# Forget-gate products before the norm factor's row in their shared bank, the first norm's chain before v's second splits, and a warm-up from a constant

## The chip, the cores and the metric

The kernel runs on one core of a Trainium2 chip. The metric is the device time of one execution in microseconds (us), as the median of several runs. Engines are named as the profile names them: PE (matrix products), PEld (its weight loads), DVE (vector), ACT (scalar), POOL (GpSimd), SP (the queue that issues most transfers).

## The reference, cut to what matters

One decoder layer over 256 tokens of 1024 channels: two attention branches in parallel, a gate that merges them, and a gated feed-forward part with a short convolution.

```python
h = rms_norm(x, attn_norm_g)
proj = h @ w_in           # qa, ka, va, qb, kb, vb, f_logit, g_logit
o_a = causal softmax attention(qa, ka, va)       # 8 heads of 64, RMS norm and partial rotation on q and k
log_f = log_sigmoid(f_logit + b_forget)          # one value per token and head
o_b = softmax(qb.kb/8 + c[t] - c[s]) vb          # c = cumsum(log_f)
gates = sigmoid(g_logit + b_gate)
x = x + (gates0 * (o_a @ w_branch_moba) + gates1 * (o_b @ w_branch_fox)) @ w_out
h2 = rms_norm(x, ffn_norm_g);  u, g = split(h2 @ w_ffn_up)
x = x + (silu(conv(g)) * u) @ w_ffn_down
```

With 256 tokens and blocks of 256 keys the first branch is plain causal attention. The factor of a token's RMS norm is one number, so the kernel multiplies it in after the products: h @ w is rs times (x * g) @ w.

## The kernel before, in words

**Products in parts.** Every large product is made three times in a fast format: a matrix is split into a rounded high part and the remainder as low part (`hi`, `lo`), and high x high, low x high and high x low are added up in PSUM. The weights stream in as `raw` tiles of 1 MB (three buffers). ACT makes the high half (L118), DVE the low half (L119), 1024 columns at a time; such a half is called a split here, and the tiles `whi` and `wlo` have six buffers each. `use` (L125) makes sure that the splits up to five places ahead are written into the program before a split is consumed. The order of the splits is: 8 of the head (`head`, which also hold x), then `qkv` in four matrices of two transfers with two splits each, then the gate and later weights. I number them from 0: 0 to 7 are the head, 8 and 9 are v's first transfer, 10 and 11 v's second, 12 to 15 q of the second branch, 16 to 19 its k, 20 to 23 its v. SP issues a transfer when the last split of the transfer three before it has been read.

**Order.** PE's order is the program's order, written out by hand (L468 to L661). On DVE, ACT, POOL and SP a planner orders the instructions by a modelled readiness and a priority, which is the place in the program; what stands in `with soon()` is taken 45 places earlier. `after(i, j)` keeps i behind j on the same engine, with no wait of its own.

**Around the change.** PE first multiplies a memset tile eight times as a warm-up (L162 to L166). Then come the 8 head steps `project_qk` (L226), the sums of squares of x (L206, in `norm1`), v (L236), q of the second branch (L236), then `turn_qk(qn, 0, 0)` (16 transposes, L284), `forget_a`, `turn_qk(kn, 0, 1)` (16 transposes, L284), and k of the second branch (L236). `norm1` computes the factor `rs` from the sums: L193 on DVE, Ln and Exp on ACT (L194), L195 to L197 on DVE. `finish_qk` needs `rs`: squares on ACT (L248), sums on DVE (L249), a chain like the norm's, products on DVE (L258) and the rotation (L265 to L268); its results `qn` and `kn` go into the transposes.

`forget_a` (L297) takes one PSUM bank of 512 columns. First `rs_row` (L428) lets PE spread `rs` over all partitions in the right half of the bank (four products, L430) and DVE copies that to `rsB` (L431), which the gates use from L451 on. Then PE makes the forget gate's products in the left half (16 matmuls, L302, from `xT`, which two SP transfers bring at L483) and DVE copies them to `fs` (L304), which `forget_b` (L311) reads. `scores` (L374) follow soon after that.

Of the kernel before, what the change touches and what calls it, by code (L numbers as in the profile page):

```python
# [8 lines left out]
F32 = mybir.dt.float32  # L9
F32R = mybir.dt.float32r  # L10
BF16 = mybir.dt.bfloat16
AF = mybir.ActivationFunctionType
ALU = mybir.AluOpType
# [4 lines left out]
P = 128  # L18
S = 256
NT = 2  # L20
D = 1024
KT = D // P
# [6 lines left out]
BIG = 1e30  # L29
HALF = 8  # L30
RB, HB, AHEAD = 3, 6, 5
NWARM = 8
SOON = 45
GAPS = (160, 96)
HEADW = S + 2 * W4
# [7 lines left out]
def decoder_block(ctx, tc, a, out):  # L43
    nc = tc.nc
# [6 lines left out]
    def T(shape, tag, bufs=1, dt=F32):  # L51
        return sb.tile(shape, dt, tag=tag, bufs=bufs, name=tag)

    def bank():
        return ps.tile([P, 512], F32, tag="bank", bufs=8, name="bank")
# [31 lines left out]
    pos = {u: i for i, u in enumerate(units)}  # L87
    split = {}
    loads = {}
    state = {"next": 0, "raw": None}  # L90

    def load(upto):
        while state["next"] <= min(upto, len(units) - 1):
            c, h = units[state["next"]]
            if c[0] == "head":
                k = c[1]
                raw = T([P, 2048], "raw", RB)
                cuts = (0, S + W4, HEADW) if k < 2 else (0, HEADW)
                for s0, s1 in zip(cuts, cuts[1:]):
                    loads[c] = nc.sync.dma_start(raw[:, s0:s1], a["head"][k][:, s0:s1])  # L100
                x, raw = raw[:, 0:S], raw[:, S:HEADW]
                split_x(k, x)
                at, n = 44, 2 if k < 2 else 1
            else:
                at, n = 44 if c[0] == "qkv" else 0, 1
                if h == 0:
                    src = a[c[0]]
                    for j in c[1:]:
                        src = src[j]
                    state["raw"] = T([P, 2048], "raw", RB)  # L110
                    loads[c] = nc.sync.dma_start(state["raw"], src)
                raw = state["raw"][:, h * 1024:(h + 1) * 1024]
            hi = T([P, 1088], "whi", HB, F32R)[:, at:at + 1024]
            lo = T([P, 1088], "wlo", HB, F32R)[:, at:at + 1024]
            w = 1024 // n
            for j in range(n):
                s = slice(j * w, (j + 1) * w)
                nc.scalar.activation(hi[:, s], raw[:, s], AF.Copy)  # L118
                nc.vector.tensor_tensor(lo[:, s], raw[:, s], hi[:, s].bitcast(F32), op=ALU.subtract)  # L119
            if c[0] == "head":  # L120
                square_x(k, x)
            split[c, h] = (hi, lo)
            state["next"] += 1

    def use(c, h):  # L125
        load(pos[c, h] + AHEAD)
        return split.pop((c, h))


# [14 lines left out]
    def split_x(k, x):  # L144
        g = g1[:, k:k + 1]
        if k == 0:
            nc.vector.tensor_scalar_mul(xh[:, k], x, g)
        else:
            nc.scalar.activation(xh[:, k], x, AF.Copy, scale=g)
        nc.vector.scalar_tensor_tensor(xl[:, k], x, g, xh[:, k].bitcast(F32), op0=ALU.mult, op1=ALU.subtract)  # L150

    def square_x(k, x):
        sq = T([P, 512], "sq", 2)[:, 0:S]
        nc.scalar.activation(sq, x, AF.Square)
        if k == 1:
            nc.gpsimd.tensor_tensor(xss[:, 1], xsq[0], sq, op=ALU.add)
        elif k > 1:
            nc.gpsimd.tensor_tensor(xss[:, k % 2], xss[:, (k + 1) % 2], sq, op=ALU.add)
        xsq.append(sq)


    warm = T([P, 512], "sq", 2, BF16)  # L162
    nc.vector.memset(warm, 0.0)
    wp = bank()
    for j in range(NWARM):
        nc.tensor.matmul(wp, warm[:, 0:P], warm, start=True, stop=True)  # L166

    load(5)
    ones1 = T([P, 1], "ones1")
    nc.vector.memset(ones1, 1.0)  # L170
    cst = T([P, 840], "cst")
    ident = cst[:, 0:128]
# [16 lines left out]
    def rsqrt_mean(dst, ss, n, shape, tag, bufs=2):  # L189

        w = T([P, 3] + shape, tag, bufs)
        v, y, t = w[:, 0], w[:, 1], w[:, 2]
        nc.vector.tensor_scalar(v, ss, 1.0 / n, EPS, op0=ALU.mult, op1=ALU.add)  # L193
        i = nc.scalar.activation(t, v, AF.Ln), nc.scalar.activation(y, t, AF.Exp, scale=-0.5)  # L194
        nc.vector.scalar_tensor_tensor(t, v, -0.5, y, op0=ALU.mult, op1=ALU.mult)  # L195
        nc.vector.tensor_tensor(t, t, y, op=ALU.mult)
        nc.vector.scalar_tensor_tensor(dst, t, 1.5, y, op0=ALU.add, op1=ALU.mult)  # L197
        return i

    rs = T([P, NT], "rs")  # L200
    rope = []

    def norm1():
        ssp = bank()
        for t in range(NT):
            nc.tensor.matmul(ssp[:, t:t + 1], xss[:, 1, t * P:(t + 1) * P], ones1, start=True, stop=True)  # L206
        rsqrt_mean(rs, ssp[:, 0:NT], D, [NT], "rsv")

        for i in range(2):
            gr = sm[:, C_GR + 16 * i:C_GR + 16 * (i + 1)][:, None, :].to_broadcast([P, NT, 16])  # L210
            rc = T([P, NT, 16], f"rc{i}")
            rsn = T([P, NT, 16], f"rsn{i}")
            nc.vector.tensor_tensor(rc, cos2[:, :, 0:16], gr, op=ALU.mult)
            nc.vector.tensor_tensor(rsn, cos2[:, :, 16:32], gr, op=ALU.mult)
            rope.append((rc, rsn))
# [4 lines left out]
    def project_qk(k, pts):  # L220
        wh, wl = use(("head", k), 0)
        for m, pt in enumerate(pts):
            rh, rl = wh[:, m * W4:(m + 1) * W4], wl[:, m * W4:(m + 1) * W4]
            for i, (lhs, rhs) in enumerate(((xh, rh), (xl, rh), (xh, rl))):
                for t in range(NT):
                    nc.tensor.matmul(pt[t], lhs[:, k, t * P:(t + 1) * P], rhs, start=(k == 0 and i == 0), stop=(k == KT - 1 and i == 2))  # L226

    def project(m, pt, h):
        for hh in range(2):
            wh, wl = use(("qkv", m - 2, h), hh)  # L230
            for k2 in range(2):
                k = 4 * h + 2 * hh + k2
                rh, rl = wh[:, k2 * 512:(k2 + 1) * 512], wl[:, k2 * 512:(k2 + 1) * 512]
                for i, (lhs, rhs) in enumerate(((xh, rh), (xl, rh), (xh, rl))):
                    for t in range(NT):
                        nc.tensor.matmul(pt[t], lhs[:, k, t * P:(t + 1) * P], rhs, start=(k == 0 and i == 0), stop=(k == KT - 1 and i == 2))  # L236
# [52 lines left out]


    gates = T([P, KT, 2, S], "gates")
    bias = T([P, NH, 384], "bias")
    cc = T([P, NT, NH], "cc")

# [1 line left out]

    def forget_a():  # L297
        fp = bank()
        rs_row(fp[:, S:])
        for k in range(KT):  # L300
            r = slice(32 * (k % 4), 32 * (k % 4 + 1))
            nc.tensor.matmul(fp[r, :S], wfg[:, k], xT[:, k], start=(k < 4), stop=(k >= 4))  # L302
        fs = T([P, 2, 384], "pT", 4)[:, 0, 0:S]
        nc.vector.tensor_copy(fs, fp[:, :S])  # L304
        fg["fs"] = fs

    def forget_b():
# [115 lines left out]
            nc.vector.tensor_tensor(ol[:, b], o2, oh[:, b].bitcast(F32), op=ALU.subtract)  # L423


    rsB = T([P, S], "rsB")

    def rs_row(rp):  # L428
        for t in range(NT):
            nc.tensor.matmul(rp[:, t * P:(t + 1) * P], rs[:, t:t + 1].to_broadcast([P, P]), ident, start=True, stop=True)  # L430
        nc.vector.tensor_copy(rsB, rp)  # L431

    def twin(kind, c, dst, mh, ml, late=False, between=None):

        for h in range(2):
            wh, wl = use((kind, c), h)
            turns = [(i, k4) for k4 in range(4) for i in range(2)] if late and h else [(i, k4) for i in range(2) for k4 in range(4)]
            for i, k4 in turns:
                o = dst[:, i * S:(i + 1) * S]
                k = 4 * h + k4  # L440
                w = slice(k4 * 256 + i * P, k4 * 256 + (i + 1) * P)
                nc.tensor.matmul(o, wh[:, w], mh[:, k], start=(k == 0 and i == 0), stop=False)  # L442
                nc.tensor.matmul(o, wh[:, w], ml[:, k], start=False, stop=False)  # L443
                nc.tensor.matmul(o, wl[:, w], mh[:, k], start=False, stop=(k == KT - 1 and i == 1))  # L444
            if h == 0 and between:
                between()
# [12 lines left out]
    def after(i, j):  # L459
        tc.add_manual_dep(i.ins, j.ins.name, mybir.DependencyInfo(mybir.DependencyClass.NoSync, mybir.DependencyReason.DATA), reason="order")  # L460
# [12 lines left out]
    with soon():  # L473
        norm1()
        qn, kn = finish_qk(0, ((0, pq), (1, pk)))
# [9 lines left out]
    with soon():  # L485
        forget_a()
# [76 lines left out]
    for c in range(4):  # L563
        for h in range(2):
# [10 lines left out]
            if c >= 2:  # L575
# [6 lines left out]
                sq = T([P, 2, S], "sq", 2)  # L582
# [146 lines left out]
```

## Time and profile before

| what | value |
|---|---|
| median of 3 runs | 368.77 us (368.7 to 369.01) |
| the profiled execution | 371.31 us |
| its span, first to last instruction | 369.5 us |
| PE busy in the span | 362.2 us (98%) |
| DVE busy | 272.5 us (74%) |
| ACT busy | 215.2 us (58%) |
| mean granted TensorE clock | 0.995 |

PE is what the time consists of: the idle time of other engines costs nothing so long as PE finds its inputs ready. So the table is read by asking where PE stands still, and where its clock is below full. A row of the timeline gives the start, the busy time, the engine, the line, output and inputs, the count, and in brackets the idle time before it with what ended it.

### The profile page before, as it was taken

The page shows a single profiled execution, that of the slowest core. Times are in us where ns is not written, and L with a number is a line of the kernel's source. Part 1 is how long each engine was busy: PE and PEld are TensorE (multiplying, and loading weights), DVE is VectorE, ACT ScalarE, POOL GpSimd, SP SyncE. Part 2 cuts the span into 40 slices and gives each one's busy share as a digit, 9 for nine tenths or more (in the row PEclk, how much of TensorE's full clock was granted, in tenths as well). Part 3 has the DMA queues.
Part 4 walks back from the last instruction along what each step waited for, and adds up shares of the span by engine and source line. Part 5 has one row for each costly group of instructions (what it writes and reads, how often), then busy time and mean ns, then how long its engine had stood idle before and what let it go on. Part 6 is the DMA issues. An engine that isn't in the chain of part 4 may idle for free.

```text
span 369.5 us, 7224 instructions
## 1 busy us (share of the span) xinstructions
PE 362.2 (98%) x2974; PEld 340.1 (92%) x2974; DVE 272.5 (74%) x472; ACT 215.2 (58%) x362; POOL 18.5 (5%) x21
## 2 busy tenths in 40 slices
PE   8999979999999999999999999999999999999996
PEld 4788857788999999999999999999999999999995
DVE  4768995993799675995889967677686767767653
ACT  4747844786547985544767746455464554545520
POOL 0550000000000000000260000000000000000000
PEclk9999999999999999999999999999999999999999
DMA  7698882427062364555455456456455545645003
GB/s 264 233 341 320 347 274 102 133 103 302 36 227 116 122 227 179 167 219 206 152 215 184 166 222 224 168 179 230 170 179 222 198 161 213 227 143 200 3 2 114
DMA packets 11425, 69.18 MB, mean 187 GB/s; under 512 B 1528, under 2 KB 1920, under 8 KB 3968
## 3 DMA queue, kind: packets, MB, share of 16 engines
q1 hardware_dynamic: 11088, 67.66, 51.0%
q10 hardware_dynamic: 304, 1.06, 0.7%
q8 instruction: 23, 0.38, 0.4%
q14 instruction: 10, 0.08, 0.1%
HBM read 67.66 MB, written 1.06 MB: 186 GB/s over the span
## 4 chain that ended last, share of the span: by engine, by line
PE 91%; DMA 3%; DVE 2%; ACT 1%; issue 1%; SPq 0%; ACTq 0%
PE bank L442 15%; PE bank L444 15%; PE bank L443 15%; PE bank L236 8%; PE bank L644 5%; PE bank L642 5%; PE bank L643 5%; PE bank L226 5%; PE bank L573 2%; PE bank L547 2%; PE bank L574 2%; PE bank L572 2%; PE bank L548 2%; PE bank L546 2%; PE bank L374 2%; DMA raw<-in_qkv 2%
## 5 line engine op out<-in xcount | busy, mean ns | idle before, releaser
L119 DVE TENSOR_TENSOR wlo<-raw,whi 128x1024 fp32r<-128x1024 f32 (+1 forms) x124 | 149.0, 1205 | 52.3 <-ACT whi L118 52.0
L118 ACT ACTIVATE whi<-raw 128x1024 fp32r<-128x1024 f32 (+1 forms) x124 | 128.6, 1044 | 86.0 <-PE bank L443 44.1
L442 PE MATMUL bank<-oh,whi 128*128 128x256 f32 x352 | 97.0, 276 | 0.0
L443 PE MATMUL bank<-ol,whi 128*128 128x256 f32 x352 | 96.8, 275 | 0.0
L444 PE MATMUL bank<-oh,wlo 128*128 128x256 f32 x352 | 96.8, 275 | 0.0
L443 PEld LDWEIGHTS bank<-ol,whi 128*128 128x128 f32 x352 | 66.1, 188 | 0.0
L442 PEld LDWEIGHTS bank<-oh,whi 128*128 128x128 f32 x352 | 66.1, 188 | 0.0
L444 PEld LDWEIGHTS bank<-oh,wlo 128*128 128x128 f32 x352 | 66.1, 188 | 0.0
L442 PE MATMUL bank<-xh,whi 128*128 128x256 f32 x128 | 36.1, 282 | 0.0
L444 PE MATMUL bank<-xh,wlo 128*128 128x256 f32 x128 | 35.3, 276 | 0.0
L443 PE MATMUL bank<-xl,whi 128*128 128x256 f32 x128 | 35.3, 276 | 0.0
L442 PEld LDWEIGHTS bank<-xh,whi 128*128 128x128 f32 x128 | 24.0, 188 | 1.1 <-PE bank L374 0.3
L443 PEld LDWEIGHTS bank<-xl,whi 128*128 128x128 f32 x128 | 24.0, 188 | 0.0
L444 PEld LDWEIGHTS bank<-xh,wlo 128*128 128x128 f32 x128 | 24.0, 188 | 0.0
L236 PE MATMUL bank<-whi,xh 128*128 128x512 f32 x64 | 20.3, 397 | 0.0
L609 DVE TENSOR_TENSOR sq<-bank,rs 128x512 f32<-128x512 f32 x22 | 15.1, 691 | 6.6 <-PE bank L444 6.5
L236 PE MATMUL bank<-whi,xl 128*128 128x512 f32 x64 | 19.7, 388 | 0.0
L236 PE MATMUL bank<-wlo,xh 128*128 128x512 f32 x64 | 19.7, 388 | 0.0
L389 ACT ACTIVATE s<-s,nm 128x128 f32<-128x128 f32 (+1 forms) x32 | 14.1, 443 | 9.0 <-DVE nm L386 9.0
L546 PE MATMUL bank<-oh,whi 128*128 128x256 f32 x64 | 17.6, 275 | 0.0
L547 PE MATMUL bank<-ol,whi 128*128 128x256 f32 x64 | 17.6, 275 | 0.0
L548 PE MATMUL bank<-oh,wlo 128*128 128x256 f32 x64 | 17.6, 275 | 0.0
(162 smaller groups left out, 735.4 us busy)
## 6 DMA issues: line engine op xcount, KB each, us to landing
raw<-in_wu SPq DMA_DIRECT2D x22, 1024.0 KB, 4.8
raw<-in_wd SPq DMA_DIRECT2D x11, 1024.0 KB, 4.8
raw<-in_qkv SPq DMA_DIRECT2D x8, 1024.0 KB, 6.7
raw<-in_wg SPq DMA_DIRECT2D x8, 1024.0 KB, 4.9
raw<-in_wb SPq DMA_DIRECT2D x4, 1024.0 KB, 4.8
raw<-in_wo SPq DMA_DIRECT2D x4, 1024.0 KB, 4.9
raw<-in_head SPq DMA_DIRECT2D x6, 640.0 KB, 4.4
xT<-in_xT SPq DMA_DIRECT2D x2, 512.0 KB, 6.9
```

Source lines behind the costliest of these rows:

```text
L118: nc.scalar.activation(hi[:, s], raw[:, s], AF.Copy)
L119: nc.vector.tensor_tensor(lo[:, s], raw[:, s], hi[:, s].bitcast(F32), op=ALU.subtract)
L226: nc.tensor.matmul(pt[t], lhs[:, k, t * P:(t + 1) * P], rhs, start=(k == 0 and i == 0), stop=(k == KT - 1 and i == 2))
L236: nc.tensor.matmul(pt[t], lhs[:, k, t * P:(t + 1) * P], rhs, start=(k == 0 and i == 0), stop=(k == KT - 1 and i == 2))
L442: nc.tensor.matmul(o, wh[:, w], mh[:, k], start=(k == 0 and i == 0), stop=False)
L443: nc.tensor.matmul(o, wh[:, w], ml[:, k], start=False, stop=False)
L444: nc.tensor.matmul(o, wl[:, w], mh[:, k], start=False, stop=(k == KT - 1 and i == 1))
L546: nc.tensor.matmul(o, wh[:, w], oh[:, 4 * br + k], start=(k == 0), stop=False)
L547: nc.tensor.matmul(o, wh[:, w], ol[:, 4 * br + k], start=False, stop=False)
L548: nc.tensor.matmul(o, wl[:, w], oh[:, 4 * br + k], start=False, stop=(k == 3))
L642: nc.tensor.matmul(o, wh[:, w], ah, start=(p == 0 and h == 0 and c == 0), stop=False)
L643: nc.tensor.matmul(o, wh[:, w], al, start=False, stop=False)
```

## The change

It has three parts. In `forget_a` the 16 products for the forget gate come first, and then the four products for the row of `rs`; both copies follow on DVE, that of the products ahead of that of the row. The function `rs_row` goes, and `rsB` is allocated earlier. In `use` the head steps write no split beyond number 9 into the program, so that splits 10 to 13 come behind `norm1` and `finish_qk` in it, and split 10 is tied behind the norm's chain: its ACT half behind Exp, its DVE half behind the last operation that gives `rs`. The warm-up reads a constant that POOL writes at the program's start, in place of a tile that DVE fills, and it has nine matmuls in place of eight.

```diff
-NWARM = 8
+NWARM = 9
...
+    rs_done = []
...
-                nc.scalar.activation(hi[:, s], raw[:, s], AF.Copy)
-                nc.vector.tensor_tensor(lo[:, s], raw[:, s], hi[:, s].bitcast(F32), op=ALU.subtract)
+                i = nc.scalar.activation(hi[:, s], raw[:, s], AF.Copy)
+                d = nc.vector.tensor_tensor(lo[:, s], raw[:, s], hi[:, s].bitcast(F32), op=ALU.subtract)
+                if (c, h) == (("qkv", 0, 1), 0):
+                    after(i, rs_done[0])
+                    after(d, rs_done[1])
...
     def use(c, h):
-        load(pos[c, h] + AHEAD)
+        load(min(pos[c, h] + AHEAD, KT + 1) if c[0] == "head" else pos[c, h] + AHEAD)
...
-    warm = T([P, 512], "sq", 2, BF16)
-    nc.vector.memset(warm, 0.0)
+    warm = nc.const_aps.tensor(1.0, (P, 512), BF16)
...
-        nc.vector.scalar_tensor_tensor(dst, t, 1.5, y, op0=ALU.add, op1=ALU.mult)
-        return i
+        d = nc.vector.scalar_tensor_tensor(dst, t, 1.5, y, op0=ALU.add, op1=ALU.mult)
+        return i + (d,)
...
-        rsqrt_mean(rs, ssp[:, 0:NT], D, [NT], "rsv")
+        rs_done.extend(rsqrt_mean(rs, ssp[:, 0:NT], D, [NT], "rsv")[1:])
...
+    rsB = T([P, S], "rsB")
...
     def forget_a():
         fp = bank()
-        rs_row(fp[:, S:])
         for k in range(KT):
             r = slice(32 * (k % 4), 32 * (k % 4 + 1))
             nc.tensor.matmul(fp[r, :S], wfg[:, k], xT[:, k], start=(k < 4), stop=(k >= 4))
+        rp = fp[:, S:]
+        for t in range(NT):
+            nc.tensor.matmul(rp[:, t * P:(t + 1) * P], rs[:, t:t + 1].to_broadcast([P, P]), ident, start=True, stop=True)
         fs = T([P, 2, 384], "pT", 4)[:, 0, 0:S]
         nc.vector.tensor_copy(fs, fp[:, :S])
+        nc.vector.tensor_copy(rsB, rp)
         fg["fs"] = fs
...
-    rsB = T([P, S], "rsB")
-
-    def rs_row(rp):
-        for t in range(NT):
-            nc.tensor.matmul(rp[:, t * P:(t + 1) * P], rs[:, t:t + 1].to_broadcast([P, P]), ident, start=True, stop=True)
-        nc.vector.tensor_copy(rsB, rp)
```

## The prediction

> **What bounds the kernel now.** I read the page's busy times first, then PE's waits, then PE's timeline around the longest of them, and last the granted clock there.
>
> ```profile
> PE 362.2 (98%) x2974; PEld 340.1 (92%) x2974; DVE 272.5 (74%) x472; ACT 215.2 (58%) x362; POOL 18.5 (5%) x21
> ```
>
> ```profile
> PE bank L302 <- DVE rsB L431: 2.4, 1, 2.4
> PE bank L166 <- DVE ones L170: 1.2, 1, 1.2
> ```
>
> PE is busy for 98% of a span of 369.5 us, and only two waits are listed for it: 1.2 us at the start and 2.4 us in the middle, at L302. So a change can only gain in three places: in one of these waits, in the tail, or in how fast PE runs while it is busy. The place of the second wait:
>
> ```profile
> 50.31 0.71 PE L284 MATMUL bank<-cst,qn 64*128 64x64 f32 x16
> 50.95 0.71 PE L430 MATMUL bank<-cst,rs 128*128 128x128 f32 x4
> 54.05 1.94 PE L302 MATMUL bank<-xT,wfg 128*32 128x256 f32 x16 [2.39 <-DVE rsB L431]
> 55.91 1.12 PE L284 MATMUL bank<-cst,qn 64*128 64x64 f32 x16
> 56.96 0.76 PE L236 MATMUL bank<-whi,xh 128*128 128x512 f32 x2
> ```
>
> ```profile
> 50.27:53.68 3.41, 1.39 (x21) 1.00 0.72 216
> 53.68:57.09 3.41, 3.04 (x33) 0.50 0.91 322
> ```
>
> After the row of `rs` (L430) PE stands for 2.39 us until DVE has copied it (L431), though L302 writes the other half of the bank. The window rows (length, PE busy, count, then the granted clock), cut where the clock changes, show a second loss: at 53.68, towards the end of the wait, the clock falls to half, and it stays there until 57.09. The same 16 transposes that took 0.64 us before the wait (50.31 to 50.95) take 1.05 us behind it (55.91 to 56.96).
>
> The copy was late because DVE worked through a backlog, and it did so up to the copy without a gap:
>
> ```profile
> 52.24 0.28 DVE L268 TENSOR_TENSOR qn<-p,p 128x128 f32<-128x128 f32 x1
> 52.44 1.21 DVE L119 TENSOR_TENSOR wlo<-raw,whi 128x1024 fp32r<-128x1024 f32 x1
> 53.58 0.41 DVE L431 COPY rsB<-bank 128x256 f32<-128x256 f32 x1
> 53.91 1.26 DVE L249 TENSOR_REDUCE ss<-sq 128x8 f32<-128x512 f32 x2
> 56.05 0.42 DVE L304 COPY pT<-bank 128x256 f32<-128x256 f32 x1 [0.87 <-PE bank L302]
> 57.09 0.17 DVE L195 SCALAR_TENSOR_TENSOR qfv<-qfv 128x16 f32<-128x16 f32 x1 [0.53 <-ACT qfv L194]
> 57.93 1.29 DVE L258 TENSOR_TENSOR qn<-bank,qf 128x512 f32<-128x512 f32 x2
> 60.67 1.23 DVE L119 TENSOR_TENSOR wlo<-raw,whi 128x1024 fp32r<-128x1024 f32 x1 [1.45 <-ACT whi L118]
> 63.10 0.36 DVE L314 SCALAR_TENSOR_TENSOR z<-bank,rs,sm 128x8 f32<-128x8 f32 x2 [1.20 <-PE bank L311]
> ```
>
> **Part 1, the order in the bank.** The products now come first and nothing of DVE's lies between them and the row. PE goes from the q transposes through L302, L430 and the k transposes into the next projection. The weight loads give the prices:
>
> ```profile
> 50.94 0.52 PEld L430 LDWEIGHTS bank<-cst,rs 128*128 128x128 f32 x4
> 54.05 0.20 PEld L302 LDWEIGHTS bank<-xT,wfg 128*32 128x32 f32 x8 [2.58 <-DVE rsB L431]
> 54.48 0.20 PEld L302 LDWEIGHTS bank<-xT,wfg 128*32 128x32 f32 x4 [0.23 <-issue]
> ```
>
> At half clock a group of four starts every 0.43 us and all 16 take 1.86 us (54.05 to 55.91); at full clock that is half, 0.93. The four of L430 take 0.52 by their loads (0.71 to the modelled end of the last). The k transposes at full clock take 0.64. So the next projection starts at 50.95 + 0.93 + 0.52 + 0.64 = 53.04 in place of 56.96: **3.9 us** earlier. Of this about 2.6 is the wait (weight loads stood 2.58), 0.9 the clock at L302 and 0.4 the clock at the transposes.
>
> Does the clock stay full? In the 3.41 us before its fall PE was busy 1.39. Against that:
>
> ```profile
> 91.24:95.14 3.90, 3.90 (x66) 1.00 0.48 202
> ```
>
> From 91.24 to 95.14 PE does nothing but small products and transposes, and the clock stays at 1.00. So it is the gap and not the smallness of the work that cost the clock, and without the gap I take it as full. The Trainium skill's "TensorE: Matmul & The Clock Gate" (Part 1) states the rule: half clock after an idle window of about 3.4 us, full clock after a busy one, and the windows run freely, not from the kernel's start. The trace agrees on the length of the window (53.68 to 57.09 is 3.41) and not on "idle": 1.39 of 3.41 us were busy.
>
> What is late next? Four things stand behind the removed wait. (a) `kn` for the second transposes, wanted at 52.4; it was ready at 52.52, so at the old time this costs 0.1, and part 2 brings it some 2 us earlier. (b) The second half of `xT`, wanted at about 51.4:
>
> ```profile
> 41.58 0.43 SPq L483 DMA_DIRECT2D xT<-in_xT  x1
> DMA to landing us min/median/max: 6.5/6.9/7.3
> 39.96 2.35 DVE L119 TENSOR_TENSOR wlo<-raw,whi 128x1024 fp32r<-128x1024 f32 x2
> ```
>
> It lands by 48.9 and has 2.5 us to spare. SP issues it behind a `qkv` transfer that waits for split 15 (the first of the two at 39.96, done near 41.2), and part 2 may push that split back; up to 2.5 us cost nothing. (c) DVE's copy of the products, which now also waits for L430; L311 wants it at 62.55 - 3.9 = 58.6, and it can run right behind the backlog, at about 53.7 to 54.1. (d) The banks for the scores, wanted 3.9 us earlier:
>
> ```profile
> 62.99 1.58 PE L374 MATMUL bank<-kT,qT 64*128 64x128 f32 x16
> ```
>
> That is 59.1. They need banks that DVE frees with L258, done at 59.2 before. DVE's chain to it saves the 0.87 us in which it stood for L302 and gets the second copy as before, so it ends near 58.4, just in time. DVE's idle time from the copy to 63.1, 0.87 + 0.53 + 1.45 + 1.20 = 4.0 us, is as large as the 3.9 us by which PE moves ahead. So I expect 0 to 0.6 us lost to a DVE that is late here, and take 0.1.
>
> **Part 2, the norm's chain first.** No instruction is added; the order changes.
>
> ```profile
> 30.07 0.15 DVE L193 TENSOR_SCALAR rsv<-bank 128x2 f32<-128x2 f32 x1
> 31.22 2.36 DVE L119 TENSOR_TENSOR wlo<-raw,whi 128x1024 fp32r<-128x1024 f32 x2 [1.00 <-ACT whi L118]
> 33.88 0.16 DVE L197 SCALAR_TENSOR_TENSOR rs<-rsv 128x2 f32<-128x2 f32 x1
> ```
>
> ```profile
> 30.12 1.06 ACT L118 ACTIVATE whi<-raw 128x1024 fp32r<-128x1024 f32 x1 [1.43 <-DMA raw<-in_qkv]
> 32.13 0.18 ACT L194 ACTIVATE rsv<-rsv 128x2 f32<-128x2 f32 x1
> ```
>
> ```profile
> 33.89 0.61 PE L236 MATMUL bank<-whi,xh 128*128 128x512 f32 x2
> 34.80 0.61 PE L236 MATMUL bank<-wlo,xh 128*128 128x512 f32 x2
> ```
>
> `rs` was ready at 34.04, as its chain stood behind splits 10 and 11 on both engines. With the chain first, Ln and Exp follow L193 at about 30.3 and 30.5, the three small operations end near 31.2, and `finish_qk` starts some 2.8 us earlier. Split 10's ACT half moves from 30.12 to about 30.7, its DVE half ends near 32.9; PE wants them at 33.89 and 34.80, so 1.9 us are left. PE spends 0.91 on a third of a split, so 2.72 on one, and split 11 may end as late as 34.80 + 2.72 = 37.5. The transfers are issued behind these splits and shift by 1 to 2 us; they are far ahead of their use (split 16, the second of the two at 39.96, ended at 42.3 and is now used at 53.0). PE waited for nothing between 28 and 50 us, so this part gains 0 by itself; it covers (a) above.
>
> **Part 3, the warm-up.**
>
> ```profile
> 1.19 3.60 PE L166 MATMUL bank<-sq 128*128 128x512 bf16 x8 [1.19 <-DVE ones L170]
> ```
>
> ```profile
> 8.36 0.30 PEld L226 LDWEIGHTS bank<-whi,xh 128*128 128x128 f32 x2 [0.50 <-ACT whi L118]
> 12.28 0.30 PEld L226 LDWEIGHTS bank<-wlo,xh 128*128 128x128 f32 x2 [0.43 <-DVE wlo L119]
> ```
>
> PE can start when the program does, some 0.4 us earlier, and the ninth matmul takes 0.45, so it ends as before. Even 0.4 us either way vanishes at 8.36 and 12.28, where PE waits for splits that wait for the head's transfers. Part 3 counts 0, with 0.4 as its bound on both sides.
>
> **The sum.** Against the profiled execution: 371.31 - 3.9 + 0.1 = 367.5 us (span 365.7). The median lies 2.54 below that execution; the same difference gives 368.77 - 3.8 = **365.0 us**. With a late DVE at its 0.6 or at nothing, and the warm-up's 0.4 for or against, it is 364.5 to 365.9.
>
> **The rivals.** *The clock was no part of the median.* Only one execution shows the fall, and whether a 2.39 us gap costs a window depends on where the windows lie. The three runs lie within 0.3 us, which speaks for every execution having it or none. If none: the wait alone goes, 368.77 - 2.5 = 366.3 us. The skill's page above, with windows that run freely, would give this in part of the executions. *A new wait takes a part*: the banks at the scores, or `xT` where split 15 slips by more than 2.5 us. The rotation's rows:
>
> ```profile
> L265 DVE TENSOR_TENSOR p<-qn,rc x2: 414/415/416, 47.4 to 50.2; 128x256 f32<-128x256 f32 x2
> L267 DVE TENSOR_TENSOR qn<-p,p x2: 278/278/279, 48.7 to 52.0; 128x128 f32<-128x128 f32 x2
> ```
>
> With two pairs like each, it is 4 x 0.41 + 4 x 0.28 = 2.8 us of DVE, and the four products L258 are 4 x 0.65 = 2.6 (by the pair at 57.93). All of this ahead of split 15 would land `xT` at 41.6 + 5.4 + 6.9 = 53.9, a wait of 2.5 us. Against: before, the planner interleaved splits and chain. Time 365.9 to 367.5. *Starved of splits, and slower*: split 11 has no tie and now stands behind all of `finish_qk` in priority. If the planner lets DVE's whole share of it (4 x 0.63 = 2.5 for L249, five small operations like L193 0.8, then 2.6 and 2.8, together 8.7 us) run ahead of split 11, this ends at 32.9 + 8.7 + 1.2 = 42.8, where PE wants it at 37.5: a stall of 5.3 against a gain of 3.8, so 370.3 us. It turns slower when split 11 ends after 41.3. Against: L249 waits for ACT's squares, and the chain for Ln and Exp, so DVE has gaps that only splits fill. *The wait stays*: if the planner had DVE copy the products before PE writes the row, PE would be kept out of the bank as now and little would change, 368.8. Against: the copy stands behind the row in the program.
>
> **How the numbers follow.** Forecast 0.55; clock no part 0.17; a new wait 0.14; starved 0.05; the wait stays 0.05; more than 4.3 us gained (a gain at the warm-up besides) 0.04. A measurement of this kernel can tell about 0.2%, 0.74 us. Faster by more: 0.55 + 0.17 + 0.13 + 0.04 = 0.89; within it 0.06; slower 0.05. The range from 364.4 to 366.9 us holds the forecast, the second case and more than half of the third, some 0.8.
>
> **What would show it.** Right: no wait of PE at L302 and none at L430, the granted clock at 1.00 from 50 to 58 us, the first L236 behind the k transposes near 53.0, `rs` (L197) near 31.2, and L374 near 59.1. Wrong: a PE wait at L374 for DVE or at L302 for `xT`; a half clock still there, which would make small work and not the gap its cause; L236 waiting for `wlo` between 34 and 50 us.

## The result, and the profile after

The changed kernel takes 367.18 us in the median of 16 runs (366.49 to 368.24), the kernel before 369.12 us in 16 runs (367.79 to 372.27). The ratio is 0.9936, with a 95% interval from 0.9914 to 0.9958: 0.64% faster, between 0.42% and 0.86%. A second series of the same two kernels, six runs against 22, gave 0.9912 (0.9885 to 0.9939). The profiled execution of the changed kernel has a span of 364.9 us against 369.5 before, so the two profiles differ by 4.6 us and the medians by 1.9 (2.4 in the second series). That difference is what most of the study is about.

PE's waits in the changed kernel (line, what it waited for, us in total, times, longest; PEq is PE's own sequencer):

```profile
PE bank L169 <- PEq L723: 0.8, 1, 0.8
PE bank L229 <- DVE xl L154: 0.3, 1, 0.3
PE bank L229 <- DVE xh L151: 0.2, 1, 0.2
```

All that is left lies at the start. The same place on PE's timeline as before, with the products for the forget gate now at L305 and the row of `rs` at L308:

```profile
49.48 0.71 PE L287 MATMUL bank<-cst,qn 64*128 64x64 f32 x16
50.12 1.07 PE L305 MATMUL bank<-xT,wfg 128*32 128x256 f32 x16
51.13 0.71 PE L308 MATMUL bank<-cst,rs 128*128 128x128 f32 x4
51.77 0.71 PE L287 MATMUL bank<-cst,qn 64*128 64x64 f32 x16
52.41 0.73 PE L239 MATMUL bank<-whi,xh 128*128 128x512 f32 x2
```

Nothing stands between the groups. From the first q transpose to the next projection it is 52.41 - 49.48 = 2.93 us, where it was 6.65. The granted clock (the number behind PE's busy time and count) is full throughout:

```profile
48.00:53.00 5.00, 5.00 (x62) 1.00 0.96 372
53.00:58.00 5.00, 5.00 (x24) 1.00 0.59 244
```

On DVE the norm's chain is early, and the two copies and the products that free the scores' banks come in time:

```profile
29.42 0.16 DVE L200 SCALAR_TENSOR_TENSOR rs<-rsv 128x2 f32<-128x2 f32 x1
...
46.65 0.29 DVE L271 TENSOR_TENSOR qn<-p,p 128x128 f32<-128x128 f32 x1
...
52.02 0.41 DVE L310 COPY pT<-bank 128x256 f32<-128x256 f32 x1
...
55.01 1.29 DVE L261 TENSOR_TENSOR qn<-bank,qf 128x512 f32<-128x512 f32 x2
```

```profile
58.41 1.58 PE L381 MATMUL bank<-kT,qT 64*128 64x128 f32 x16
```

`kn` is ready at 46.9, long before its transposes at 51.77, and L261 ends at 56.3, where the scores (L381) start at 58.41. The rest of the 4.6 us lies ahead of all this: the q transposes start at 49.48 and not at 50.31.

### The profile page after: what moved, and what is told of

Read it like the earlier page. It is cut to its first block, busy times and chain, and to the rows that moved or that the text cites. A ratio compares the mean times of both kernels' runs of the same rounds, so it can differ in the third digit from the quotient of the medians.

```text
span 364.9 us, 7223 instructions
## 1 busy us (share of the span) xinstructions
PE 359.9 (99%) x2975; PEld 339.5 (93%) x2975; DVE 272.3 (75%) x471; ACT 215.3 (59%) x362; POOL 18.6 (5%) x21
## 4 chain that ended last, share of the span: by engine, by line
PE 97%; DMA 1%; DVE 0%; issue 0%; ACT 0%; DVEq 0%
PE bank L443 15%; PE bank L445 15%; PE bank L444 15%; PE bank L239 12%; PE bank L229 6%; PE bank L645 5%; PE bank L643 5%; PE bank L644 5%; PE bank L574 2%; PE bank L548 2%; PE bank L575 2%; PE bank L573 2%; PE bank L549 2%; PE bank L547 2%; PE bank L381 2%; PE bank L425 2%
```

## The experiments

I had two theories of the difference between profiles and medians. The first: the wait is there in every execution, but a window at half clock is paid in some only, and the profiled execution before was one of these. The rival: a part of the gain belongs to the norm's chain or to the warm-up, so that the order in the bank alone gives less. Every execution's mean granted clock is recorded beside its time, which lets the first theory be counted. In the runs of the kernel before beside the experiments it reads so (the first series ran beside the first four experiments, the second beside the last four):

| kernel before | executions | median us |
|---|---|---|
| first series, mean clock 0.998 or more | 22 of 33 | 369.15 |
| first series, mean clock 0.995 or less | 11 of 33 | 371.06 |
| second series, 0.998 or more | 13 of 22 | 369.02 |
| second series, 0.995 or less | 9 of 22 | 371.26 |

There is nothing between 0.995 and 0.998. One window of 3.41 us at half clock is 0.46% of the span, so a mean near 0.995 is one lost window. Some 36% of the executions (20 of 55) lose one, that is, run one window at half clock, and take about 2 us more. The execution of 371.31 us that the prediction worked from had 0.995.

**The order in the bank alone.** The kernel before with the last part of the diff:

```diff
         fp = bank()
-        rs_row(fp[:, S:])
         for k in range(KT):
...
+        rp = fp[:, S:]
+        for t in range(NT):
+            nc.tensor.matmul(rp[:, t * P:(t + 1) * P], rs[:, t:t + 1].to_broadcast([P, P]), ident, start=True, stop=True)
...
+        nc.vector.tensor_copy(rsB, rp)
```

> The kernel before with the new order in the shared bank alone (old warm-up, old place of the norm's chain). If the order in the bank is the whole gain, PE has no wait at the forget products, the first projection behind the k transposes starts 3.7 to 3.9 us after the q transposes' end less than before, and the time is 0.990 to 0.995 of before, as with the whole change (0.9936). If the norm's chain or the warm-up carries a part, the time is above 0.9965, and the profile shows PE waiting at the k transposes or at the scores for DVE.

Measured: 367.32 us (366.58 to 369.05, 10 runs) against 369.45, ratio 0.9932 (0.9907 to 0.9958), no execution under 0.998. PE's timeline in it:

```profile
49.35 0.71 PE L284 MATMUL bank<-cst,qn 64*128 64x64 f32 x16
49.99 1.07 PE L302 MATMUL bank<-xT,wfg 128*32 128x256 f32 x16
50.99 0.71 PE L305 MATMUL bank<-cst,rs 128*128 128x128 f32 x4
51.63 0.72 PE L284 MATMUL bank<-cst,qn 64*128 64x64 f32 x16
52.28 0.73 PE L236 MATMUL bank<-whi,xh 128*128 128x512 f32 x2
```

The same 2.93 us. Part 1 is the whole gain that these runs can tell, and the q transposes start as early here (49.35) as in the changed kernel, with the old warm-up.

**The norm's chain alone.**

```diff
+                if (c, h) == (("qkv", 0, 1), 0):
+                    after(i, rs_done[0])
+                    after(d, rs_done[1])
...
-        load(pos[c, h] + AHEAD)
+        load(min(pos[c, h] + AHEAD, KT + 1) if c[0] == "head" else pos[c, h] + AHEAD)
```

> The kernel before with the norm's chain ahead of v's second splits alone. If it only rearranges work that PE does not wait for, 0.999 to 1.001, with rs ready some 2.5 us earlier and PE's wait at the forget products still 2 to 2.5 us. If it lets DVE reach the copy of the row earlier, that wait shrinks below 1.5 us and the time falls by 0.9 us or more (0.9975). If splits starve PE, PE waits for wlo between 34 and 50 us and the time is above 1.002.

Measured: 369.34 us (367.99 to 371.88, 12 runs), ratio 0.9986 (0.9957 to 1.0015), three of 12 with 0.995 or less. `rs` comes early, and the wait stays:

```profile
30.84 0.16 DVE L201 SCALAR_TENSOR_TENSOR rs<-rsv 128x2 f32<-128x2 f32 x1
...
48.27 4.63 DVE L120 TENSOR_TENSOR wlo<-raw,whi 128x1024 fp32r<-128x1024 f32 x4
52.82 0.42 DVE L435 COPY rsB<-bank 128x256 f32<-128x256 f32 x1
```

```profile
51.01 0.71 PE L434 MATMUL bank<-cst,rs 128*128 128x128 f32 x4
53.29 1.07 PE L306 MATMUL bank<-xT,wfg 128*32 128x256 f32 x16 [1.57 <-DVE rsB L435]
```

DVE does the attention's chain earlier and then four splits in a row, and the copy again stands at the backlog's end. PE waits 1.57 us, which looks like a gain on the 2.39 of before; but the unchanged kernel shows 1.67 in its second profile, below.

**The warm-up alone.**

```diff
-NWARM = 8
+NWARM = 9
...
-    warm = T([P, 512], "sq", 2, BF16)
-    nc.vector.memset(warm, 0.0)
+    warm = nc.const_aps.tensor(1.0, (P, 512), BF16)
```

> The kernel before with the warm-up from a constant and nine matmuls alone. If the head is bound by its transfers, 0.999 to 1.001. If the 0.8 us by which the head's products ended earlier in the changed kernel's profile (27.2 against 28.0) come from the earlier full clock, 0.9975 to 0.9985, and a profile in which the full clock comes a window earlier or PE does not wait at the second head step.

Measured: 370.66 us (368.38 to 373.28, 12 runs), ratio 1.0014 (0.9986 to 1.0042); seven of 12 executions have 0.995 or less. No gain can be measured, and the profile shows what an early PE is worth while the copy is late: PE reaches the row at 50.18, where it was 50.95, and the forget products start where they did before.

```profile
50.18 0.71 PE L429 MATMUL bank<-cst,rs 128*128 128x128 f32 x4
53.95 1.93 PE L301 MATMUL bank<-xT,wfg 128*32 128x256 f32 x16 [3.05 <-DVE rsB L430]
```

**The gap filled.** Eight matmuls into a spare bank, read by nobody, where PE waits (they multiply a zeroed tile `keep`, whose allocation is left out here):

```diff
         rs_row(fp[:, S:])
+        kp = bank()
+        for j in range(8):
+            nc.tensor.matmul(kp, keep[:, 0:P], keep, start=True, stop=True)
```

> The kernel before with eight bf16 matmuls of 512 columns into a spare bank put between the row and the forget products, in the time in which PE waits; what they compute is read by nobody. If the gap costs the clock, the clock stays at 1.00 from 50 to 58 us, the 16 forget products take 0.9 us in place of 1.9 and the k transposes 0.64 in place of 1.05, and the wait itself stays: the profile gains 1.3 us, the median 0.4 to 1.3 us (0.9965 to 0.999), as not every execution need lose a window. If the small products and transposes cost the clock and not the gap, it falls all the same and the ratio is 0.9995 to 1.001.

Measured: 369.01 us (368.34 to 372.27, 12 runs), ratio 0.9984 (0.9956 to 1.0012), and none of 12 under 0.998.

```profile
50.29 0.71 PE L435 MATMUL bank<-cst,rs 128*128 128x128 f32 x4
51.05 1.67 PE L304 MATMUL bank<-keep 128*128 128x512 bf16 x7
52.66 1.07 PE L307 MATMUL bank<-xT,wfg 128*32 128x256 f32 x16
```

The row shows seven of the eight fillers; the record of one is missing, its weight load is there. The forget products take 1.0 us and the clock stays: it is the gap that costs it, not the small work. The ratio alone would not show this, since its interval holds 1; the count does, 0 of 12 lost windows against 20 of 55. The median equals that of the kernel before's executions which lost no window (369.15), as it should, since the time of the wait is still spent. In this profile the fillers ended later than the copy (52.15), so PE lost some 0.5 us to them; if that holds in other executions, the ratio understates the clock's part.

**A bank of its own for the row**, in the old order:

```diff
-        rs_row(fp[:, S:])
+        rs_row(bank()[:, 0:S])
```

> The kernel before in its old order, but with the row of rs in a bank of its own, so that its copy and the forget products share none. If sharing the bank made PE wait, the wait at the forget products goes without any reordering and the time is that of part 1 alone: 0.9932 of before, 0.991 to 0.996, and no execution falls under a mean clock of 0.997. If PE waited for DVE's backlog in another way, or the further bank in use makes a new wait, the time stays above 0.998.

Measured: 367.35 us (367.06 to 367.54, six runs) against 369.55, ratio 0.9919 (0.989 to 0.9949), no execution under 0.998.

```profile
50.64 0.71 PE L430 MATMUL bank<-cst,rs 128*128 128x128 f32 x4
51.28 1.07 PE L302 MATMUL bank<-xT,wfg 128*32 128x256 f32 x16
```

So the cause was the shared bank: PE was held for the copy of the other half only where the two shared one. Which way the copy is taken off the path does not matter: 367.35 here, 367.32 for the order, 367.18 and 367.12 for the whole change. Whether the chip itself needs this order, or only the program's ordering by banks asks for it, no run here tests.

**The copy made later.** Two more copies of the row ahead of the one that counts, read by nobody:

```diff
+        junk = T([P, S], "junk")
+        for j in range(2):
+            nc.vector.tensor_copy(junk, rp)
         nc.vector.tensor_copy(rsB, rp)
```

> The kernel before with two further copies of the row on DVE, ahead of the one that PE waits for and read by nobody; with a sum that DVE puts between them the copy ends 1.3 us later. PE's wait grows from about 2.4 to 3.7 us. If a window of 3.41 us is lost when the wait fills more than some 2.3 us of it, and windows lie anywhere, then the share of executions with a mean clock under 0.997 grows from 11 in 33 to about (3.41 + 3.7 - 4.7) / 3.41 = 0.7, and the time is 1.3 us longer by the wait and 0.5 to 0.7 us by the clock: 1.004 to 1.006. If the clock falls for another cause than the gap, the share stays near a third and the time is 1.0035 or less.

Measured: 372.57 us (370.23 to 375.14, 12 runs), ratio 1.0062 (1.0033 to 1.0092). Eleven of 12 executions have 0.995 or less, six of them 0.990. A later copy loses windows more often, as the theory says; 0.990 is about two windows. The share of 0.7 was too low, because the limit of 2.3 us of waiting in one window that I took was too high (the last section has what the profiles give). The profiled execution, with 371.25 us one of the shorter, shows the copy 1.26 us behind the first extra one, as forecast:

```profile
52.02 0.42 DVE L433 COPY junk<-bank 128x256 f32<-128x256 f32 x1
...
53.28 0.41 DVE L434 COPY rsB<-bank 128x256 f32<-128x256 f32 x1
```

```profile
53.75 1.07 PE L302 MATMUL bank<-xT,wfg 128*32 128x256 f32 x16 [2.27 <-DVE rsB L434]
```

But DVE's backlog ended early in it, so PE waits 2.27 us there and not the 3.7 of the forecast; how long it waited in the other eleven was not profiled. PE's busy time and the clock by window:

```profile
51.53:54.94 3.41, 1.19 (x22) 1.00 0.87 308
54.94:58.36 3.42, 3.42 (x22) 0.50 0.37 156
```

**Both kernels once more.** No edit. The kernel before:

> The kernel before, unchanged, for a second profile of it and more executions. Ratio 0.997 to 1.003. If the start of the forget products is set by DVE and not by PE, they start near 54.0 us again, whatever time PE reaches the row; a third of the executions has a mean clock under 0.997, and these take 1.3 to 2 us longer than the others.

Measured: 369.17 us (367.76 to 371.32, 12 runs), ratio 0.9988 (0.9961 to 1.0016); four of 12 have 0.995, at 370.51 to 371.32 us, the other eight 367.76 to 369.44. The profiled execution (369.44 us) lost no window:

```profile
50.28 0.71 PE L284 MATMUL bank<-cst,qn 64*128 64x64 f32 x16
50.93 0.71 PE L430 MATMUL bank<-cst,rs 128*128 128x128 f32 x4
53.31 1.07 PE L302 MATMUL bank<-xT,wfg 128*32 128x256 f32 x16 [1.67 <-DVE rsB L431]
54.31 0.71 PE L284 MATMUL bank<-cst,qn 64*128 64x64 f32 x16
54.95 0.73 PE L236 MATMUL bank<-whi,xh 128*128 128x512 f32 x2
```

The forget products start at 53.31 and not near 54.0: the end of DVE's backlog moves by 0.7 us between these two executions. From the first q transpose to the projection it is 4.67 us.

The changed kernel:

> The changed kernel, unchanged, for a second profile of it on the same chip as the others. 0.991 to 0.996. No execution with a mean clock under 0.997; the time from the first q transpose to the next projection is 2.9 us again, while the start of the q transposes moves with the head's transfers by up to 1 us and takes the time with it.

Measured: 367.12 us (366.56 to 367.4, six runs), ratio 0.9912 (0.9885 to 0.9939), none under 0.998. The q transposes start at 49.91 here, and the stretch is 52.84 - 49.91 = 2.93 us again:

```profile
49.91 0.71 PE L287 MATMUL bank<-cst,qn 64*128 64x64 f32 x16
...
52.84 0.73 PE L239 MATMUL bank<-whi,xh 128*128 128x512 f32 x2
```

## Why the prediction was right, and where its sum was not

The direction, the place and the mechanism were right; the size was not. A gain of 3.8 us was forecast and the medians differ by 1.9, half of it. The range from 364.4 to 366.9 us is 0.988 to 0.995 of the 368.77 from which it was worked out, and the measured 0.9936 lies in it; as a bare time, 367.18 us lies 0.3 above its upper end and 2.2 above the point, as the kernel before itself came out 0.35 longer. That the range held it is owed to a rival whose time it took in, and not to the sum, whose own bounds ended at 365.9 (0.992); so far it is luck. Step by step:

- **The stretch at the bank.** Forecast 3.9 us less, measured 6.65 - 2.93 = 3.72 less in the profiled execution. The forget products take 1.01 us at full clock (0.93 forecast), the row 0.64 (0.52; the modelled end of 0.71 was nearer than the loads).
- **The step that failed** is the one from the profiled execution to the median: "The median lies 2.54 below that execution; the same difference gives 368.77 - 3.8". It took the difference as a constant of the measurement. In fact the profiled execution was one of the 36% that lose a window and it had a long wait besides. The profiled one without that loses 4.67 - 2.93 = 1.74 us at the bank, the one with it 3.72; the clock's part of the 1.98 between them is (1.86 - 1.00) + (1.05 - 0.64) = 1.27, the wait's part 2.39 - 1.67 = 0.72. Weighted with the shares, 0.64 x 1.74 + 0.36 x 3.72 = 2.5 us is an estimate, from two profiles, of what the mean of many executions gains; over the 16 runs each the means differ by 369.61 - 367.25 = 2.4 us. The medians gain 1.9 there and 2.4 in the second series. The executions before that lost no window have medians of 369.15 and 369.02, some 1.9 us above the 367.18 and 367.12 of after, and the third that lost one pulls the median of all up by a few tenths more.
- **The rival that was nearest** was the one in which the clock is no part of the median, 366.3 us, given 0.17. Its gain of 2.5 us was still a little high, as not every execution waits for 2.4 us. The evidence for the forecast against it was three times within 0.3 us; in the longer series the kernel before spreads over 4.5 us.
- **The clock rule.** The Trainium skill's "TensorE: Matmul & The Clock Gate" (Part 1) says that the windows run freely, not from the kernel's start. The runs agree: the clock first rises between 3.70 us (the changed kernel) and 7.16 us (the later copy) after the start, and by that rule a gap costs a window in only a part of the executions, as it did in 20 of 55.
- **What is late next.** None of the four: no PE wait at `kn`, at `xT`, at the copy of the products or at the scores. DVE had more room than forecast: L261 ends at 56.3, where 58.4 was expected for it, and `kn` was in time even without part 2 (order alone). Two more signs came earlier than named: `rs` is ready at 29.58 (31.2 forecast; 31.00 with part 2 alone) and the scores start at 58.41 (59.1).
- **Parts 2 and 3 count 0.** Neither alone differs from 1 by more than its interval, and the order alone is as good as all three. That they are worth nothing at all is not shown: 0.1% would not be seen, and alone they stand ahead of a late copy that hides what they may gain.
- **The head.** In the profiles the head's products ended 0.8 us earlier after the change. The order alone and the unchanged kernel's second profile show the same early end with the old warm-up, so it does not need part 3. Whether part 3 helps where the clock first rises late stays open: with the warm-up alone the rise was at 5.84 us and the head's products ended at 27.2, in the first profile before at 5.86 and 28.0.

## What to carry to other kernels

When a producer and a consumer share a PSUM bank, look at what the copy between them queues behind: putting the independent products first, or giving the small row a bank of its own, takes another engine's backlog off PE's path, here at no cost that the runs show. Before costing a clock loss, take several executions: a profile shows one of them, and if its own time stands out from the runs, the difference may be the very effect that is being priced. When the times spread less after a change, as here (1.8 us from the lowest to the highest against 4.5), look whether it took away a cost that only some executions pay; the mean then gains more than the median.

## What the runs showed of the hardware

Here a gap of about 2 us cost more than itself. The clock fell behind windows of 3.41 us in which PE was busy 1.4 us (the profiled execution before) and 1.19 us (the later copy). It did not fall behind these two, of the norm's chain alone and of the unchanged kernel's second profile. No change of the clock marks their edges there: they are counted on in steps of 3.41 us from the first rise of the clock in the same profile.

```profile
50.38:53.79 3.41, 1.84 (x33) 1.00 1.01 382
```

```profile
49.62:53.03 3.41, 2.02 (x24) 1.00 0.69 231
```

The counting can be checked where two changes are seen. In the first profile before, the clock rises at 5.86 and falls at 53.65, which is 14 steps of 3.413 us; with a bank of its own for the row it rises at 6.79 and falls behind the last work at 365.19, which is 105 steps. Counted on to the end of PE's work, the same profile before has a closer case. The first row is the window of the fall, the second the one in which PE's work ends, and the third shows the clock still full after that:

```profile
50.23:53.65 3.42, 1.43 (x21) 1.00 0.72 216
364.26:367.67 3.41, 1.58 (x14) 1.00 0.66 230
367.67:369.50 1.83, 0.00 (x0) 1.00 0.01 1
```

So here the limit lies between 1.43 and 1.58 us of busy time in a window, 42% and 46%, by the profile's modelled ends of matmuls. Put the other way, 1.98 us of standstill within one window cost the clock, and 1.83 us did not.
